# One 512-column matmul for both parts of x in the feed forwards' up products, and the bank's two halves added

## The chip, the cores and the metric

The kernel runs on one core of a Trainium2 chip. The metric is device time in microseconds from launch to end, the median of several runs. TensorE multiplies matrices and writes to PSUM, VectorE and ScalarE work elementwise, GpSimd does a few small operations, SyncE issues all DMA transfers.

## What is computed

A row of 256 tokens of width 1024 goes through three layers: differential attention with a pooling mixer, sliding window attention, and a block with a convolution module and gated attention. Four feed forwards of width 2816 belong to them; the first two convolve the up products over three tokens, the last two do not and add half of their result. The change touches these:

```python
def conv_glu_ffn(x, norm_g, w_up, conv_w, conv_b, w_down):
    S = x.shape[1]
    h = rms_norm(x, norm_g) @ w_up
    hp = jnp.pad(h, ((0, 0), (CONV_W - 1, 0), (0, 0)))
    c = conv_b
    for j in range(CONV_W):
        c = c + conv_w[j] * hp[:, j:j + S]
    gate, up = jnp.split(c, 2, axis=-1)
    return x + (jax.nn.silu(gate) * up) @ w_down

def swiglu_ffn(h, w13, w2):
    gate, up = jnp.split(h @ w13, 2, axis=-1)
    return (jax.nn.silu(gate) * up) @ w2
```

All of it is float32.

## The kernel before

**Products in parts.** Float32's accuracy comes from splitting. A weight chunk of 128x2048 is loaded by SyncE into one of two staging buffers `st` (line 175), ScalarE casts it to `whi` (line 191, two pieces of 1024 columns), and VectorE writes the remainder `wlo` (line 195, four pieces of 512). The normed and transposed x exists as two parts in the same way. A product is then three matmuls into one accumulation: first part by first part, first by second, second by first. `mm3` (lines 244 to 246) does this with tokens on the output's partitions and up to 512 columns of weights; `mm_w` (lines 462 to 464) does it with weights stationary and the 256 tokens as columns.

**Stream.** `Stream` holds five chunks of split weights. A chunk's buffer is released when TensorE has used it, then the next chunk is split into it and the staging buffer is loaded again. Its splitting has a low priority in the scheduler. A feed forward uses 22 chunks of up weights and 11 of down weights, in the order up, up, down in its steady part.

**Feed forward.** The up products are made in 22 blocks `f` of 128 gate columns and 128 up columns (the two halves `s`). Blocks 0 to 2 are "leads": made with tokens on partitions through `mm3`, copied to SBUF and transposed into a PSUM tile each (line 373). Blocks 3 to 21 come from `up_mm`: for each half, eight row blocks of x, three matmuls of 256 columns each. Both halves of a block stand in one PSUM tile `up` of 512 columns, that is one bank; the pool `ps` has four. `glu` then works on both halves: in the feed forwards with a convolution, ScalarE (line 398) and two VectorE steps (lines 399 and 401) a half, all reading `up`; then silu (407), product (409) and the two parts of `g` (413 and 414). Without a convolution silu and product read `up` themselves. After each second block, `down` multiplies two blocks of g by a down chunk into four accumulators `dn`: 24 matmuls of 512 columns. The last three chunks' down products come at the end, first for token block 0, then for token block 1, with the next stage's norm between them.

**Order.** Tiles are drawn from pools with a fixed number of buffers, and a scheduler puts the instructions of each engine into one fixed order, in which the engine then runs them; an instruction waits for semaphores of others. The pool `u` (`u288`, five buffers) gives the convolution's `c`.

## Time and profile before

| | us |
|---|---|
| median of three runs | 1078.18 |
| the three runs | 1079.1, 1074.94, 1078.18 |
| the profiled execution, first to last instruction (span) | 1077.6 |
| TensorE busy in it | 1052.6 |
| VectorE busy | 730.2 |
| ScalarE busy | 562.4 |

The profile is of one execution. Its span is the only time that is known of it. TensorE's matmuls overlap in the records, so its busy time and the mean of one matmul are longer than the share of the time that a matmul takes; distances between starts are free of that.

### The profile page before, as it was taken

How to read it: one execution, taken by the hardware profiler on the slowest of the kernel's cores; microseconds unless marked ns; L12 is line 12 of the kernel's file. 1: busy time of each engine (PE TensorE's matmuls, PEld its weight loads, DVE VectorE, ACT ScalarE, POOL GpSimd, SP SyncE). 2: the span in 40 equal slices, each digit the busy share in tenths (PEclk: the TensorE clock that was granted, in tenths of full speed). 3: DMA queues.
4: the chain of work that ended last, by engine and by line, in shares of the span. 5: the costliest groups of instructions: out<-in, count | busy, mean ns of one | idle time of the engine just before them, and what ended most of it. 6: DMA issues, size and time to landing. Idle time of an engine off the chain costs nothing.

```text
span 1077.6 us, 17590 instructions
## 1 busy us (share of the span) xinstructions
PE 1052.6 (98%) x7078; PEld 959.0 (89%) x7078; DVE 730.2 (68%) x1526; ACT 562.4 (52%) x953; POOL 32.0 (3%) x40
## 2 busy tenths in 40 slices
PE   5999999999999999999999999999999999999997
PEld 4778999999887898999999999999888889999996
DVE  5786787677867569777676555545799896545542
ACT  5575655555557457555555434433544566434431
POOL 1100000000021000000000000000000010000000
PEclk9999999999999999999999999999999999999999
DMA  6754565555453074555545555554613166555531
GB/s 248 249 192 157 182 229 195 182 180 189 157 176 118 1 248 167 205 186 192 195 158 186 203 184 190 195 180 173 203 71 118 40 215 235 194 183 174 193 118 39
DMA packets 28449, 185.82 MB, mean 172 GB/s; under 512 B 3280, under 2 KB 4176, under 8 KB 7120
## 3 DMA queue, kind: packets, MB, share of 16 engines
q1 hardware_dynamic: 28368, 184.71, 49.0%
q8 instruction: 55, 0.90, 0.3%
q14 instruction: 26, 0.21, 0.1%
HBM read 183.65 MB, written 1.05 MB: 171 GB/s over the span
## 4 chain that ended last, share of the span: by engine, by line
PE 88%; DVE 5%; DMA 4%; ACT 2%; issue 0%; POOL 0%; SPq 0%; POOLq 0%; ACTq 0%; DVEq 0%
PE up L464 13%; PE up L463 13%; PE up L462 13%; PE dn L244 7%; PE dn L245 7%; PE dn L246 7%; DMA st<-in_w 3%; PE sc L555 2%; PE op L244 2%; PE op L246 2%; PE op L245 2%; DVE wlo L195 2%; PE lead L246 2%; PE lead L244 2%; PE lead L245 2%; DVE ys L1008 2%
## 5 line engine op out<-in xcount | busy, mean ns | idle before, releaser
L195 DVE TENSOR_TENSOR wlo<-st,whi 128x512 fp32r<-128x512 f32 x668 | 435.4, 686 | 231.2 <-ACT whi L191 230.6
L191 ACT CAST whi<-st 128x1024 fp32r<-128x1024 f32 x334 | 342.6, 1046 | 316.2 <-PE up L463 180.6
L462 PE MATMUL up<-xT,whi 128*128 128x256 f32 x1216 | 344.6, 283 | 0.0
L464 PE MATMUL up<-xT,wlo 128*128 128x256 f32 x1216 | 344.1, 283 | 0.0
L463 PE MATMUL up<-xT,whi 128*128 128x256 f32 x1216 | 344.1, 283 | 0.0
L462 PEld LDWEIGHTS up<-xT,whi 128*128 128x128 f32 x1216 | 233.2, 192 | 1.3
L463 PEld LDWEIGHTS up<-xT,whi 128*128 128x128 f32 x1216 | 233.3, 192 | 1.2
L464 PEld LDWEIGHTS up<-xT,wlo 128*128 128x128 f32 x1216 | 233.2, 192 | 0.1
L244 PE MATMUL dn<-whi,g 128*128 128x512 f32 x352 | 137.9, 392 | 0.9 <-ACT g L413 0.9
L245 PE MATMUL dn<-wlo,g 128*128 128x512 f32 x352 | 137.4, 390 | 0.0
L246 PE MATMUL dn<-whi,g 128*128 128x512 f32 x352 | 137.2, 390 | 0.0
L246 PEld LDWEIGHTS dn<-whi,g 128*128 128x128 f32 x352 | 66.1, 188 | 15.1 <-DVE g L414 1.0
L244 PEld LDWEIGHTS dn<-whi,g 128*128 128x128 f32 x352 | 66.2, 188 | 13.8 <-ACT g L413 1.1
L245 PEld LDWEIGHTS dn<-wlo,g 128*128 128x128 f32 x352 | 66.2, 188 | 12.1
L398 ACT ACTIVATE c<-up,pv 128x256 f32<-128x256 f32 x88 | 49.6, 564 | 31.8 <-DVE c L401 27.2
L244 PE MATMUL lead<-whi,xT 128*128 128x256 f32 x192 | 55.3, 288 | 0.0
L246 PE MATMUL lead<-whi,xT 128*128 128x256 f32 x192 | 54.3, 283 | 0.0
L245 PE MATMUL lead<-wlo,xT 128*128 128x256 f32 x192 | 54.3, 283 | 0.0
L244 PE MATMUL proj<-whi,xT 128*128 128x512 f32 x112 | 46.1, 412 | 2.1 <-ACT xT L264 2.1
L246 PE MATMUL proj<-whi,xT 128*128 128x512 f32 x112 | 45.3, 404 | 0.3 <-DVE xT L265 0.3
L399 DVE SCALAR_TENSOR_TENSOR c<-up,pv,c 128x255 f32<-128x255 f32 x88 | 42.0, 477 | 4.4 <-ACT c L398 3.8
L1008 DVE SCALAR_TENSOR_TENSOR ys<-u,dwh,ys 128x240 f32<-128x240 f32 (+29 forms) x109 | 44.9, 460 | 0.1
(210 smaller groups left out, 1342.1 us busy)
## 6 DMA issues: line engine op xcount, KB each, us to landing
st<-in_up SPq DMA_DIRECT2D x88, 1024.0 KB, 4.9
st<-in_dn SPq DMA_DIRECT2D x44, 1024.0 KB, 4.8
st<-in_w SPq DMA_DIRECT2D x22, 1024.0 KB, 5.3
gb<-in_rows SPq DMA_DIRECT2D x10, 512.0 KB, 4.0
st<-in_w0o SPq DMA_DIRECT2D x4, 1024.0 KB, 5.0
st<-in_w1o SPq DMA_DIRECT2D x4, 1024.0 KB, 4.8
st<-in_w2o SPq DMA_DIRECT2D x4, 1024.0 KB, 4.8
st<-in_w SPq DMA_DIRECT2D x2, 512.0 KB, 8.0
```

The costliest lines, as they stand in the source:

```text
L191: A.copy(hi[:, c], st[:, c])
L195: V.tensor_sub(lo[:, c], st[:, c], hi[:, c].bitcast(F32))
L244: T.matmul(o, l[0], r[0], start=first, stop=False)
L245: T.matmul(o, l[0], r[1], start=False, stop=False)
L246: T.matmul(o, l[1], r[0], start=False, stop=last)
L398: A.activation(c, ps, AF.Identity, bias=PVs(cb, blk), scale=PVs(cw, 3 * blk + 2))
L399: V.scalar_tensor_tensor(c[:, 1:], ps[:, :S - 1], PVs(cw, 3 * blk + 1), c[:, 1:], ALU.mult, ALU.add)
L462: T.matmul(o, w[0], x[0], start=first, stop=False)
L463: T.matmul(o, w[0], x[1], start=False, stop=False)
L464: T.matmul(o, w[1], x[0], start=False, stop=last)
L555: T.matmul(o, qT[r0:r0 + 64, qb, :], kT[r0:r0 + 64, kb, 0:L], start=True, stop=extra is None)
L1008: V.scalar_tensor_tensor(y[:, k:], self.u[:, :S - k], self.w(k), y[:, k:], ALU.mult, ALU.add)
```

## The change

x's two parts become one tile with the parts side by side for every row block, so that 512 columns, 256 of each part, stand in a row. In `up_mm` each half gets a PSUM tile of its own. One matmul of 512 columns takes the weights' first part by both parts of x, into both halves of the bank; one of 256 columns adds the weights' second part by x's first part to the bank's first half. `join` then copies the bank's second half to SBUF on ScalarE and adds the first half to it on VectorE; `glu` reads these tiles `h` from SBUF. The `h` come from the pool `u`, with its five buffers as before. The leads, the down products and every other product keep their three matmuls; `mm_w` only takes its operand in another form. Lines move by 10 to 27.

```diff
+class Parts(tuple):
+    def __new__(cls, t):
+        self = super().__new__(cls, (t[:, :, 0, :], t[:, :, 1, :]))
+        self.t = t
+        return self
+    def both(self, ko):
+        return self.t[:, ko, :, :]
...
     def new_T(name):
-        return tuple(
-            act.tile([P, KD, S], F32R, tag=f"xT{k}", name=f"{name}{k}") for k in range(2)
-        )
+        return Parts(act.tile([P, KD, 2, S], F32R, tag="xT", name=name))
...
         def up_mm(self, f, mid=None):
-            o = self.ups[f] = ps_t("up").rearrange("p (s t) -> p s t", s=2)
+            hs = []
             w = v3(W.get(self.up, f), KD)
             for s in range(2):
                 if s and mid is not None:
                     mid()
+                o = ps_t("up")
                 for ko in range(KD):
-                    mm_w(o[:, s, :], cut(w, slice(None), ko, slice(s * P, (s + 1) * P)),
-                         cut(self.xT, slice(None), ko, slice(0, S)), ko == 0, ko == KD - 1)
+                    mm_both(o, cut(w, slice(None), ko, slice(s * P, (s + 1) * P)), self.xT, ko, ko == 0, ko == KD - 1)
+                hs.append(join(o))
             W.free((self.up, f))
-            self.glu(f)
-
-        def glu(self, f):
-            pu = self.ups.pop(f)
+            self.glu(f, hs)
+
+        def glu(self, f, hs=None):
+            if hs is None:
+                pu = self.ups.pop(f)
+                hs = [pu[:, s, :] for s in range(2)]
...
-                    ps = pu[:, s, :]
+                    ps = hs[s]
...
-                cs = [pu[:, s, :] for s in range(2)]
+                cs = hs
...
-    def mm_w(o, w, x, first, last):
+    def mm_w(o, w, xT, ko, first, last):
+        x = cut(xT, slice(None), ko, slice(0, S))
         T.matmul(o, w[0], x[0], start=first, stop=False)
         T.matmul(o, w[0], x[1], start=False, stop=False)
         T.matmul(o, w[1], x[0], start=False, stop=last)
+
+    def mm_both(o, w, xT, ko, first, last):
+        T.matmul(o, w[0], xT.both(ko), start=first, stop=False, skip_group_check=True)
+        T.matmul(o[:, :S], w[1], xT[0][:, ko, :], start=False, stop=last, skip_group_check=True)
+
+    def join(o):
+        h = u288("h")[:, :S]
+        A.copy(h, o[:, S:])
+        V.tensor_tensor(h, o[:, :S], h, ALU.add)
+        return h
```

The instructions' order shows it first on TensorE, at block 3 of the first feed forward, around the transposes of lead block 2 between its two halves. The first is the kernel before; the numbers in the names tell buffers apart.

```order
L463 MATMUL up_1207<-xT1_699,whi_899 128x256
L464 MATMUL up_1207<-xT0_698,wlo_902 128x256
L373 MATMUL up_1134<-cc_78,lead_1138 128x128 x2
L462 MATMUL up_1207<-xT0_698,whi_899 128x256
L463 MATMUL up_1207<-xT1_699,whi_899 128x256
```

The changed kernel at the same place on TensorE:

```order
L483 MATMUL up_1203<-xT_696,whi_896 128x512
L484 MATMUL up_1203<-xT_696,wlo_899 128x256
L383 MATMUL up_1130<-cc_78,lead_1134 128x128 x2
L483 MATMUL up_1240<-xT_696,whi_896 128x512
L484 MATMUL up_1240<-xT_696,wlo_899 128x256
```

The second half goes to a tile of its own, `up_1240`, the fifth of this pool since the leads; it takes the bank of lead block 0.

On ScalarE, in the steady part of the first feed forward, two successive blocks before (`c0` and `c1` are the two halves' convolution starts):

```order
L398 ACTIVATE c0_1575<-up_1516,pv_81 128x256
L191 CAST whi_1565<-st_1466 128x1024 x2
L398 ACTIVATE c1_1579<-up_1516,pv_81 128x256
L407 ACTIVATE sl_1583<-c0_1575 128x256
L413 CAST g_1587<-m_1585 128x256
L398 ACTIVATE c0_1649<-up_1590,pv_81 128x256
L191 CAST whi_1639<-st_1514 128x1024 x2
```

And two successive blocks on ScalarE in the changed kernel:

```order
L489 COPY h_1828<-up_1811 128x256
L203 CAST whi_1801<-st_1696 128x1024 x2
L489 COPY h_1848<-up_1831 128x256
L411 ACTIVATE c0_1861<-h_1828,pv_81 128x256
L411 ACTIVATE c1_1865<-h_1848,pv_81 128x256
L203 CAST whi_1851<-st_1761 128x1024 x2
L420 ACTIVATE sl_1869<-c0_1861 128x256
L489 COPY h_1893<-up_1876 128x256
L426 CAST g_1873<-m_1871 128x256
L489 COPY h_1913<-up_1896 128x256
```

Each half's copy now stands in the queue where the half ends, between the weight casts and the steps of `glu`, which read `h` in SBUF.

## Rows read from the trace of the kernel before

**Rows 1.** The page: TensorE's busy time, its granted clock by slices, the chain's shares.
```profile
PE 1052.6 (98%) x7078; PEld 959.0 (89%) x7078; DVE 730.2 (68%) x1526; ACT 562.4 (52%) x953; POOL 32.0 (3%) x40
...
PEclk9999999999999999999999999999999999999999
...
PE 88%; DVE 5%; DMA 4%; ACT 2%; issue 0%; POOL 0%; SPq 0%; POOLq 0%; ACTq 0%; DVEq 0%
```

**Rows 2.** Busy us of each engine by stretch, granted clock, DMA: two feed forwards.
```profile
125.00:285.00 160.00, 160.00 (x1128) 150.39 (x1127) 123.35 (x244) 92.20 (x144) 0.00 (x0) 1.00 0.55 190
...
592.00:755.00 163.00, 163.00 (x1142) 153.29 (x1141) 86.05 (x158) 69.75 (x101) 0.55 (x1) 1.00 0.54 187
```

**Rows 3.** Timeline of TensorE, first feed forward: start us, duration us, instruction.
```profile
196.77 0.40 PE L244 MATMUL dn<-whi,g 128*128 128x512 f32 x1
...
202.01 0.39 PE L246 MATMUL dn<-whi,g 128*128 128x512 f32 x1
202.24 0.28 PE L462 MATMUL up<-xT,whi 128*128 128x256 f32 x1
...
213.75 0.40 PE L244 MATMUL dn<-whi,g 128*128 128x512 f32 x1
```

**Rows 4.** Groups by line and shape: count, busy us, mean ns, idle before.
```profile
L462 PE MATMUL up<-xT,whi 128*128 128x256 f32 x1216 | 344.6, 283 | 0.0
...
L407 ACT ACTIVATE sl<-up 128x256 f32<-128x256 f32 x44 | 16.4, 379 | 7.9 <-PE up L464 7.8
...
L409 DVE TENSOR_TENSOR m<-up,sl 128x256 f32<-128x256 f32 x44 | 18.2, 418 | 7.7 <-ACT sl L407 7.7
...
L195 DVE TENSOR_TENSOR wlo<-st,whi 128x512 fp32r<-128x512 f32 x668 | 435.4, 686 | 231.2 <-ACT whi L191 230.6
...
L191 ACT CAST whi<-st 128x1024 fp32r<-128x1024 f32 x334 | 342.6, 1046 | 316.2 <-PE up L463 180.6 <-PE dn L246 61.3 <-DMA st<-in_w 27.6
...
L398 ACT ACTIVATE c<-up,pv 128x256 f32<-128x256 f32 x88 | 49.6, 564 | 31.8 <-DVE c L401 27.2 <-PE up L464 4.4
...
L413 ACT CAST g<-m 128x256 fp32r<-128x256 f32 x88 | 35.4, 404 | 16.0 <-DVE m L409 16.0
```

**Rows 5.** Timeline, first feed forward's start: block 3's products, block 0's last read, a wait.
```profile
122.61 0.36 PE L462 MATMUL up<-xT,whi 128*128 128x256 f32 x1
...
125.49 0.48 DVE L401 SCALAR_TENSOR_TENSOR c<-up,pv,c 128x254 f32<-128x254 f32 x1
...
129.18 0.19 PEld L246 LDWEIGHTS dn<-whi,g 128*128 128x128 f32 x1 [0.34 <-DVE g L414]
```

**Rows 6.** Timeline, second feed forward's start: the same places, with g's second part.
```profile
402.44 0.48 DVE L401 SCALAR_TENSOR_TENSOR c<-up,pv,c 128x254 f32<-128x254 f32 x1
...
405.64 0.42 DVE L414 TENSOR_TENSOR g<-m,g 128x256 fp32r<-128x256 f32 x1
...
406.12 0.19 PEld L246 LDWEIGHTS dn<-whi,g 128*128 128x128 f32 x1 [0.46 <-DVE g L414]
```

**Rows 7.** Timeline, first feed forward's end: last up product, first down product, a wait.
```profile
276.09 0.28 PE L464 MATMUL up<-xT,wlo 128*128 128x256 f32 x1
276.21 0.40 PE L244 MATMUL dn<-whi,g 128*128 128x512 f32 x1
...
283.39 0.19 PEld L246 LDWEIGHTS dn<-whi,g 128*128 128x128 f32 x1 [0.16 <-DVE g L414]
```

**Rows 8.** Weight stream, first feed forward: issues, a cast, landing us, ScalarE's waits.
```profile
195.51 0.33 SPq L175 DMA_DIRECT2D st<-in_up  x1
...
206.42 6.40 SPq L175 DMA_DIRECT2D st<-in_up  x2
...
202.44 1.05 ACT L191 CAST whi<-st 128x1024 fp32r<-128x1024 f32 x1 [1.19 <-PE dn L246]
...
st<-in_up SPq DMA_DIRECT2D x88, 1024.0 KB, 4.9
...
ACT whi L191 <- PE up L463: 30.1, 12, 3.3
```

More of the change, by code (lines that the diff above doesn't have):

```diff
@@ L979, in conv_in @@
                 mm_w(ag[j][:, s, :], cut(w, slice(None), ko, slice(s * P, (s + 1) * P)),
-                     cut(xT, slice(None), ko, slice(0, S)), ko == 0, ko == KD - 1)
+                     xT, ko, ko == 0, ko == KD - 1)
         W.free(("w2", j))
@@ L1031, in forget_sums @@
         for ko in range(KD):
-            mm_w(o, cut(flw, slice(None), ko), cut(xT, slice(None), ko, slice(0, S)), ko == 0, ko == KD - 1)
+            mm_w(o, cut(flw, slice(None), ko), xT, ko, ko == 0, ko == KD - 1)
         z, cum = (tmp.tile([P, S], F32, tag="sl", name=n)[:8, :] for n in ("z", "cum"))
@@ L1064, in proj_qk @@
             mm_w(o[:, :S], cut(v3(W.get("w2", 4 + 2 * s + ko // 4), 4), slice(None), ko % 4, slice(b * P, (b + 1) * P)),
-                 cut(xT, slice(None), ko, slice(0, S)), ko == 0, ko == KD - 1)
+                 xT, ko, ko == 0, ko == KD - 1)
         A.activation((q2, k2)[s][:, b, :], o[:, :S], AF.Copy, scale=1.0 if s else -0.125)
```

## The prediction

> **What bounds the kernel now.** I read the head of the page first [rows 1]: TensorE is busy 98% of the span, its granted clock is at full speed (the 2.4 GHz level) in all forty slices, and the chain that ended last runs 88% on it, with the three lines of the up products at the front of the list of lines. Busy time alone does not make an engine the bound here, since matmuls overlap and their ends are modelled, so I next read two feed forwards as stages [rows 2]. In the first TensorE has no idle time in 160 us, while VectorE is busy 77% and ScalarE 58%; in the third, which has no convolution, the others are at 53% and 43%. So in the feed forwards, some 640 of the 1078 us, the rate of the matmuls sets the time, and everything else has room.
>
> The mean of one up matmul, 283 ns in the groups by line [rows 4], is a duration in an overlapped pipeline and is of no use for a sum. The distance between starts is, and the timeline of TensorE gives it [rows 3]. Twenty-four down matmuls of 512 columns start between 196.77 and 202.24 us: 5.47 us, 227.9 ns each. Ninety-six up matmuls of 256 columns start between 202.24 and 213.75 us: 11.51 us, 119.9 ns each. Two equations, 512a + b = 227.9 and 256a + b = 119.9, give a = 0.4219 ns for a column (2.37 columns a ns, close to the clock) and b = 11.9 ns for each matmul whatever its width. That b is what the change can save, and only there.
>
> **What the change saves.** Each group of three 256-column matmuls on one weight block becomes one of 512 columns (first part of the weights, both parts of x) and one of 256 (second part of the weights, first part of x). The columns that stream stay 768. There are 1216 such groups (the count of line 462 [rows 4]: 4 feed forwards x 19 blocks x 2 halves x 8 row blocks). Before: 3 x 119.9 = 359.7 ns. After: 227.9 + 119.9 = 347.8 ns. Saved: 11.9 ns x 1216 = 14.5 us. Trains of one width are all that rows 3 measure, but the changes of width are there too: 512 followed by 256 takes 0.23 us (202.01 to 202.24 [rows 3]) and 256 followed by 512 takes 0.12 us (276.09 to 276.21 [rows 7]), so a mixed pair should cost the sum of its parts, and not more. One weight load of the three goes as well; it overlaps the matmuls before and after, so I price it at nothing beyond b. Bounds on the term: nothing, if an alternating pair costs what three did, and 29 us, if the pair's shorter matmul loses its b as well; I take 14.5 us, from the rows that measure both widths. A loss is excluded by the 0.23 and 0.12 us.
>
> The Trainium skill, page "TensorE: Matmul & The Clock Gate", section "Back-to-back issue gap", gives the warm gap as the columns at 2.4 GHz plus about 2.5 ns. By that rule b is 2.5 and the change saves an estimated 1216 x 2.5 = 3.0 us, which would leave the time near 1075 us; the trace does not agree, with 11.9 ns.
>
> **What the change adds.** Per half, a ScalarE copy out of the bank's second 256 columns and a VectorE addition of the first: 152 of each. Nearest rows [rows 4]: the silu that reads 128x256 from PSUM takes 379 ns, the product that takes one operand from PSUM and one from SBUF takes 418 ns. A feed forward gets 38 of each: ScalarE + 14.4 us, VectorE + 15.9 us. In the first feed forward's stage that makes VectorE 123.35 + 15.9 = 139 of about 156 us (89%) and ScalarE 107 of 156 (68%): off the path, since neither reaches the bound, but with less room. What covers it is the queue of finished work ahead of TensorE. The order of the DMA issues, of GpSimd's instructions and of those of the stages between the feed forwards stays as it was, so there I change nothing.
>
> **Banks.** Before, a block's two halves share one of four PSUM banks, which comes free after the last of the convolution's reads; now each half has a bank of its own, which comes free after its copy and its addition. TensorE therefore comes back to a bank after three more halves, 3 x 8 x 347.8 ns = 8.3 us, where it had three whole blocks, over 17 us. In the steady order the copy follows a half directly or stands behind two convolution starts, a pair of weight casts and a silu (2 x 564, 2 x 1046, 379 ns [rows 4]), and the addition behind one or two weight subtractions (686 ns each): 3.6 + 0.4 + 1.4 + 0.4 = 5.8 us at most. That fits 8.3 us, so I price it at nothing.
>
> It does not fit at the start of the two feed forwards with a convolution. There the first three blocks still hold three banks, the first half of block 3 takes the fourth, and its second half needs the bank of block 0, which six operations must first read; before, the second half went on in its own bank. In the first feed forward the products of block 3 start at 122.61 us and the last read of block 0 ends at 125.49 + 0.48 = 125.97 us [rows 5]. Sixteen matmuls (2.78 us) and two transposes end at about 125.6, so TensorE waits some 0.4 us, starts the second half at 126.0 and the down products at 128.8. The third of these started at 129.18 before, already behind the same VectorE result [rows 5]; now it is about 129.26. In the second feed forward block 0 is read until 402.44 + 0.48 = 402.92 us [rows 6]; the second half then runs to 405.7, and the third down product, held before until 406.12 by the second part of g (405.64 + 0.42 = 406.06), comes at 406.2. So the two starts lose about 0.1 us each and the 0.19 us that block 3 would have saved: 0.6 us together. Without a convolution two operations read a lead's bank, and I see no wait.
>
> **The end of a feed forward** gets shorter, not longer. Block 21's last product starts at 276.09 us; the second part of its g releases a weight load at 283.39, which has waited 0.16 us for it [rows 7]. After the change the first half's join runs beside the second half. Behind the last product ScalarE has the copy, a convolution start, a cast of g, a weight cast and the second convolution start (0.38 + 0.56 + 0.40 + 1.05 + 0.56 = 2.95 us [rows 4]); VectorE then two convolution steps (0.48 each [rows 5]), two weight subtractions and the product (2.75 us in all), and last come the cast of g and its subtraction, 0.82 us: 6.5 us against 7.1 us. I take 0.16 us off.
>
> **The sum**, against the profiled execution: 1077.6 - 14.5 + 0.6 - 0.2 = 1063.5 us of span. The median of the three runs is 0.6 us above that span, so the forecast is 1064 us.
>
> **The rivals.**
> First, the pair saves nothing: the fixed part hangs on changing between widths or on the long matmul's doubled operand, and 512 + 256 columns take the 359.7 ns that three matmuls took. Then only the starts' 0.2 us are left and the time is about 1078 us, no change. Against it stand the two changes of width above, at 0.23 and 0.12 us; for it, that no train of alternating pairs is in the trace. The Trainium skill's rule of "Back-to-back issue gap", with its fixed part of 2.5 ns, leads to nearly the same place; the 11.9 ns speak against it.
>
> Second, a slower kernel: the bank hand-over takes the matmuls' place as the bound. The place is the copy in ScalarE's queue. A weight cast waits there for TensorE to finish with an older chunk, 12 times by line 463 in the first feed forward and up to 3.3 us at once [rows 8]; a copy behind it waits too. 3.3 + 2.1 for the pair of casts + 0.4 copy + two subtractions 1.4 + 0.4 addition is 7.6 us, 0.7 short of the 8.3 at which TensorE starts to stand. A pair of convolution starts ahead of the copy (2 x 0.56 us) makes it 8.7: 0.4 us at half of the 152 halves is 30 us, and the time 1094 us. The gain is gone from 0.1 us per half on. Against it: the waits of ScalarE for TensorE end with the very product that the copy behind them needs, or an earlier one, so they are mostly not added to the copy's own wait.
>
> Third, half the gain: the weight stream falls behind. One staging buffer goes round in 206.42 - 195.51 = 10.9 us [rows 8]: issued at 195.51, landed 4.9 us later at 200.4, its cast starts at 202.44 on a release by TensorE, 2.0 us of room. Two chunks now take 0.25 us less, and a join in the stretch from cast to last subtraction adds about 0.8 us, so 1 us of room stays; if two or three joins fall there (2.1 us), each round is 0.3 us late, 16 rounds make 5 us in a feed forward. The five live chunks absorb that in part, so I put this case at 3 to 9 us lost, 1067 to 1073 us.
>
> Fourth, more gain than 15 us, if the 256-column matmul in the pair hides its fixed part wholly under the long one: twice 14.5 us, 1049 us. Nothing in rows 3 asks for it.
>
> **How the numbers follow.** Forecast (1061 to 1067 us) 0.76; half the gain 0.10; nothing saved 0.06; slower by the banks 0.05; twice the gain 0.03. The kernel's own three runs lie between 1074.9 and 1079.1 us, so I let the lower end of the forecast go down by 2 us, to 1059; the upper end, 1071, takes in the better half of the third rival. What is left out is 0.03 + 0.06 + 0.05 + 0.05 = 0.19. A measurement of this kernel tells about 0.5% (5.4 us) from no change, so faster means below 1072.8 us: 0.76 + 0.03 + 0.08 = 0.87. No change: 0.06 + 0.02 = 0.08. Slower: 0.05.
>
> **What would show it.** In the changed kernel's timeline one half's matmuls should start 2.78 us behind the other's, with about 228 ns after each 512-column matmul and 120 ns after each 256-column one; 240 ns after the long one would be the first rival. TensorE should show no wait for the additions in the steady part of any feed forward, and one of about 0.4 us and 1.6 us ahead of the second half of block 3 in the first and second feed forward; waits of the up products for VectorE all along would be the second rival, and casts that wait for a DMA of up or down weights in place of TensorE the third. VectorE's busy time should rise by about 64 us and ScalarE's by about 58. The stretches between the feed forwards should keep their lengths. What would make the prediction wrong is a fixed part that is not b of rows 3, or a copy that regularly reaches its bank more than 8 us late.

## The result

| | before | after |
|---|---|---|
| median, us | 1077.56 (1074.94 to 1079.1, 5 runs) | 1070.18 (1069.44 to 1073.31, 5 runs) |
| ratio, 95% interval | | 0.9939, 0.9922 to 0.9956 |
| span of the profiled execution, us | 1077.6 | 1070.6 |
| VectorE busy, us | 730.2 | 777.9 |
| ScalarE busy, us | 562.4 | 619.1 |

The kernel became 0.6% faster. The direction was right, and the time lies just inside the stated range; the size was not right: 7 us came where 14 were forecast. What follows is about the missing half.

The page after answers to [rows 1] with TensorE's busy line, its granted clock (nine tenths or more, the level of 2.4 GHz, in all slices but one, which shows eight) and the chain:

```profile
PE 1046.3 (98%) x5862; PEld 894.8 (84%) x5862; DVE 777.9 (73%) x1678; ACT 619.1 (58%) x1105; POOL 32.0 (3%) x40
...
PEclk9999999999999999999999999999998999999999
...
PE 87%; DVE 5%; DMA 3%; ACT 2%; issue 1%; POOL 1%; SPq 0%; POOLq 0%; ACTq 0%; DVEq 0%
```

TensorE executes 1216 matmuls fewer and still sets the time. The two stretches of [rows 2], as the busy time of each engine after (us, PE, PEld, DVE, ACT, POOL, then clock, DMA share, GB/s):

```profile
125.00:285.00 160.00, 159.04 (x831) 135.14 (x830) 134.02 (x283) 106.10 (x185) 0.00 (x0) 1.00 0.55 190
592.00:755.00 163.00, 163.00 (x850) 138.74 (x849) 102.32 (x199) 86.46 (x140) 0.55 (x1) 1.00 0.54 186
```

VectorE has 134 of 160 us to do in the first and ScalarE 106, both below the span, as the prediction had it. In the third feed forward TensorE has no idle time at all. So the answer lies in its rate. The timeline of TensorE at the entry of a group of pairs, in the same feed forward as [rows 3] (start us, duration us, instruction):

```profile
184.66 0.39 PE L258 MATMUL dn<-whi,g 128*128 128x512 f32 x1
184.88 0.39 PE L483 MATMUL up<-xT,whi 128*128 128x512 f32 x1
185.11 0.28 PE L484 MATMUL up<-xT,wlo 128*128 128x256 f32 x1
185.22 0.40 PE L483 MATMUL up<-xT,whi 128*128 128x512 f32 x1
185.45 0.28 PE L484 MATMUL up<-xT,wlo 128*128 128x256 f32 x1
185.57 0.40 PE L483 MATMUL up<-xT,whi 128*128 128x512 f32 x1
185.81 0.28 PE L484 MATMUL up<-xT,wlo 128*128 128x256 f32 x1
185.93 0.40 PE L483 MATMUL up<-xT,whi 128*128 128x512 f32 x1
```

From 184.88 to 185.93 us three pairs take 1.05 us. The trace holds the starts in nanoseconds, and there one pattern repeats every three pairs: 241 and 119, 236 and 113, 233 and 117 ns behind the long and the short matmuls, 1059 ns in all, 353 a pair. (Distances below a nanosecond here and below are means over many such starts.) Before, three matmuls took 360.0 ns. So 7 ns a pair were saved, and not 11.9.

The length of the stages, read from TensorE's starts: first lead product to first down product, from there to the last up product, from there to the last down product.

| us | before, feed forwards 1 to 4 | after |
|---|---|---|
| start | 25.17, 26.24, 25.18, 25.18 | 26.22, 25.49, 24.99, 25.54 |
| steady part | 147.45, 147.68, 147.24, 147.24 | 145.52, 145.53, 145.52, 145.54 |
| end | 17.20, 17.21, 17.13, 16.24 | 17.32, 17.33, 17.14, 16.23 |

The steady parts give 7.5 us, the starts lose 0.5 and the ends 0.2; the rest of the span is 0.2 us shorter. Of the 7.5 us some 0.6 are waits and not rate: before, the first two steady parts were 0.2 and 0.4 us longer than the other two, with the waits for g of [rows 5] and [rows 6] in them, and after all four are equal. The steady part is the finest measure there is of the change: in the changed kernel it repeats to 0.02 us over four feed forwards, where the stretch between the third and the fourth took anything from 118.7 to 124.5 us in the profiles of this study, whatever the kernel, and moves single times by some us.

The groups by line that answer to [rows 4] (count, busy us, mean ns, idle before):

```profile
L483 PE MATMUL up<-xT,whi 128*128 128x512 f32 x1216 | 431.4, 399 | 1.5 <-DVE c L414 1.2
L484 PE MATMUL up<-xT,wlo 128*128 128x256 f32 x1216 | 341.7, 281 | 0.0
...
L489 ACT COPY h<-up 128x256 f32<-128x256 f32 x152 | 55.8, 367 | 56.8 <-PE up L484 56.6
L490 DVE TENSOR_TENSOR h<-up,h 128x256 f32<-128x256 f32 x152 | 63.7, 419 | 10.2 <-ACT h L489 10.0
L203 ACT CAST whi<-st 128x1024 fp32r<-128x1024 f32 x334 | 343.1, 1048 | 176.9 <-PE up L483 66.0 <-PE dn L258 42.0 <-DMA st<-in_up 20.1
```

The joins cost ScalarE 55.8 and VectorE 63.7 us, and neither the up products nor the casts show a wait for them that matters: all 2432 matmuls of both lines waited 1.5 us together.

### The profile page after: what moved, and what is told of

The parts are those of the page before. It is cut to its first block, busy times and chain, and to the rows that moved or that the text cites. A ratio compares the mean times of both kernels' runs of the same rounds, so it can differ in the third digit from the quotient of the medians.

```text
span 1070.6 us, 15476 instructions
## 1 busy us (share of the span) xinstructions
PE 1046.3 (98%) x5862; PEld 894.8 (84%) x5862; DVE 777.9 (73%) x1678; ACT 619.1 (58%) x1105; POOL 32.0 (3%) x40
## 3 DMA queue, kind: packets, MB, share of 16 engines
HBM read 183.65 MB, written 1.05 MB: 173 GB/s over the span
## 4 chain that ended last, share of the span: by engine, by line
PE 87%; DVE 5%; DMA 3%; ACT 2%; issue 1%; POOL 1%; SPq 0%; POOLq 0%; ACTq 0%; DVEq 0%
PE up L483 26%; PE up L484 13%; PE dn L256 8%; PE dn L258 7%; PE dn L257 7%; PE sc L582 2%; DVE wlo L207 2%; DMA st<-in_w 2%; PE proj L256 2%; PE proj L258 2%; PE proj L257 2%; PE o L841 1%; PE op L256 1%; PE op L257 1%; PE op L258 1%; DMA st<-in_up 1%
## 5 line engine op out<-in xcount | busy, mean ns | idle before, releaser
L207 DVE TENSOR_TENSOR wlo<-st,whi 128x512 fp32r<-128x512 f32 x668 | 441.6, 686 | 179.6 <-ACT whi L203 178.9
L483 PE MATMUL up<-xT,whi 128*128 128x512 f32 x1216 | 431.4, 399 | 1.5 <-DVE c L414 1.2
L483 PEld LDWEIGHTS up<-xT,whi 128*128 128x128 f32 x1216 | 228.6, 188 | 58.0 <-issue 1.6
L484 PEld LDWEIGHTS up<-xT,wlo 128*128 128x128 f32 x1216 | 230.3, 189 | 1.3
L489 ACT COPY h<-up 128x256 f32<-128x256 f32 x152 | 55.8, 367 | 56.8 <-PE up L484 56.6
L256 PEld LDWEIGHTS dn<-whi,g 128*128 128x128 f32 x352 | 66.1, 188 | 14.5 <-ACT g L426 0.6
L490 DVE TENSOR_TENSOR h<-up,h 128x256 f32<-128x256 f32 x152 | 63.7, 419 | 10.2 <-ACT h L489 10.0
L426 ACT CAST g<-m 128x256 fp32r<-128x256 f32 x88 | 35.5, 406 | 28.3 <-DVE m L422 28.3
L284 ACT ACTIVATE junk<-x 128x512 bf16<-128x512 f32 x32 | 20.2, 631 | 47.2 <-DVE x L323 26.1
L411 ACT ACTIVATE c<-h,pv 128x256 f32<-128x256 f32 x76 | 45.8, 603 | 2.4 <-DVE h L490 2.4
```

Of the source, the lines that this page charges most:

```text
L207: V.tensor_sub(lo[:, c], st[:, c], hi[:, c].bitcast(F32))
L256: T.matmul(o, l[0], r[0], start=first, stop=False)
L411: A.activation(c, ps, AF.Identity, bias=PVs(cb, blk), scale=PVs(cw, 3 * blk + 2))
L426: A.copy(hi, m)
L483: T.matmul(o, w[0], xT.both(ko), start=first, stop=False, skip_group_check=True)
L484: T.matmul(o[:, :S], w[1], xT[0][:, ko, :], start=False, stop=last, skip_group_check=True)
```

## The experiments

Theories at the start: **A**, changing between widths costs TensorE time that trains of one width don't show; **B**, the long matmul's operand or x's new layout costs; **C**, the traffic of the joins to and from PSUM slows the matmuls. Each run has the kernel before beside it on the same chip, at medians of 1076.5 to 1078.4 us.

### Runs of eight and of sixteen (e1_runs8, e2_runs16)

The same matmuls in another order: eight long ones, then eight short ones in each half; then sixteen long ones into two banks, then sixteen short ones (block 3 stays in pairs there).

```diff
                 for ko in range(KD):
-                    mm_both(o, ...)
+                    mm_long(o, cut(w, ...), self.xT, ko, ko == 0)
+                for ko in range(KD):
+                    mm_short(o, cut(w, ...), self.xT, ko, ko == KD - 1)
```

Expected of eight:

> The changed kernel with the order inside each half altered: eight 512-column matmuls in a row, then eight of 256 columns. Same matmuls, loads, banks and joins. Theory A, a change of width costs: in the changed kernel a 512-column matmul between two of 256 takes 236 ns and the short one 117 ns, 353 ns a pair; in the down products, the first long ones after a run of short ones take 233, 236, 228, 233, 231 ns and then settle at 227. So the long ones here should mean some 230 ns and the short ones 120, 350 ns a pair, and the time should fall by about 1216 x 3 ns = 4 us, to 1066 us. Theory B, the long matmul of the up products costs 236 ns by its own operands (x as the moving operand, both parts, one bank's two halves): every long one stays at 236, the time stays at 1070 us. Theory C, the joins' traffic slows the matmuls: as B, 1070 us.

Expected of sixteen:

> The changed kernel with both halves of a block taken together (all but block 3): sixteen 512-column matmuls into two banks, then sixteen of 256 columns, then the two joins. Theory A, change of width: fewer changes than with runs of eight, long ones mean some 228.5 ns, 348.5 ns a pair over 1152 pairs, about 5.5 us less than the changed kernel, 1064.5 us, unless the later join of the first half makes a wait. Theories B and C: 353 ns a pair, 1070 us, no gain over the changed kernel.

Measured: 1064.84 us (ratio 0.989, 0.9859 to 0.9922) and 1062.82 us (0.9888, 0.9834 to 0.9942). The steady parts are 143.96 and 143.61 us. Timeline of TensorE, runs of eight; equal matmuls in a row are one row with their count:

```profile
250.99 1.98 PE L483 MATMUL up<-xT,whi 128*128 128x512 f32 x8
252.80 1.12 PE L486 MATMUL up<-xT,wlo 128*128 128x256 f32 x8
253.76 2.00 PE L483 MATMUL up<-xT,whi 128*128 128x512 f32 x8
255.60 1.11 PE L486 MATMUL up<-xT,wlo 128*128 128x256 f32 x8
```

Runs of sixteen:

```profile
189.04 3.82 PE L490 MATMUL up<-xT,whi 128*128 128x512 f32 x16
192.69 0.52 PE L493 MATMUL up<-xT,wlo 128*128 128x256 f32 x3
```

The view of the runs of sixteen ends inside its second run.

The run at 250.99 us comes straight from down products, which are 512 wide too: eight in 1.81 us, 226 ns each. The next one, behind short ones, takes 1.84 us. In means by position the long ones take 232, 233, 228, 231, 230 ns and then 226.7 for as long as the run lasts; the short ones 113, 119 and then 120.0. The whole comes to 348.4 ns a pair in runs of eight and 347.2 in runs of sixteen. The operands and the joins are as in the changed kernel, and with runs of eight the banks too, so the order alone is worth 5 to 7 us. The same long matmul runs at 226.7 ns here, so B's operand falls.

### The layout alone, and no joins (e3_layout, e4_nojoin)

The kernel before with x's parts side by side in one tile; and the changed kernel without the joins, which leaves the product of the weights' first part and x's second part out of blocks 3 to 21.

```diff
     def new_T(name):
-        return tuple(
-            act.tile([P, KD, S], F32R, tag=f"xT{k}", name=f"{name}{k}") for k in range(2)
-        )
+        return Parts(act.tile([P, KD, 2, S], F32R, tag="xT", name=name))
```

```diff
-                hs.append(join(o))
+                hs.append(o[:, :S])
```

> The kernel before with one thing of the change: the two parts of x side by side in one tile. Three 256-column matmuls, one bank for both halves, no join. If the layout slowed the reads of x (a part of theory B), the 256-column matmuls would take more than the 120 ns of the kernel before, and 3 x 1216 of them at, say, 122 ns would add 7 us, 1085 us. Theories A and C: 120 ns, no change from the kernel before, 1077.6 us.

> The changed kernel without its joins: the silu and the convolution read the bank's first half, so the product of the weights' first part by x's second part is left out of the result. TensorE's instructions and banks are the same; 152 copies and 152 additions are gone. Theory C, the joins' traffic slows the matmuls: the pair falls from 353 to some 347 ns, the time by 7 us to 1063 us. Theories A and B: the pair stays at 353 ns and the time within 1 us of the changed kernel's, 1069.5 us, with what is left from the starts of the feed forwards.

Measured: 1078.38 us (0.9994, 0.9976 to 1.0011) and 1071.32 us (0.9945, 0.9924 to 0.9966). Timeline of TensorE with the layout alone, three matmuls apart:

```profile
188.69 0.28 PE L472 MATMUL up<-xT,whi 128*128 128x256 f32 x1
...
189.05 0.28 PE L472 MATMUL up<-xT,whi 128*128 128x256 f32 x1
```

And without joins, one pair:

```profile
188.90 0.40 PE L483 MATMUL up<-xT,whi 128*128 128x512 f32 x1
189.14 0.28 PE L484 MATMUL up<-xT,wlo 128*128 128x256 f32 x1
189.25 0.40 PE L483 MATMUL up<-xT,whi 128*128 128x512 f32 x1
```

The three matmuls take 0.36 us as before (120.0 ns each), and the steady parts without joins are 145.52, 145.54, 145.52 and 145.52 us, those of the changed kernel to 0.02. B's layout and C fall.

### Two equal widths, and 512 with 384 (e5_wide, e9_384)

Is it the change of width, or the alternation of two weight blocks behind a 512-column matmul? Both kernels widen the second matmul only, and so add products of the two second parts.

```diff
-        T.matmul(o[:, :S], w[1], xT[0][:, ko, :], ...)
+        T.matmul(o, w[1], xT.both(ko), ...)
```

```diff
-        T.matmul(o[:, :S], w[1], xT[0][:, ko, :], ...)
+        T.matmul(o[:, : S + P], w[1], xT.both(ko).rearrange("p a s -> p (a s)")[:, : S + P], ...)
```

> Both matmuls of a pair 512 columns wide: the second one takes the weights' second part by both parts of x, which adds the product of the two second parts that the other kernels leave out. In the up products and the down products no matmul has another width than the one before it; the stationary block still alternates between the weights' first and second part. Theory A (a change of width costs): 226.7 to 228 ns between all starts, as in the trains of the down products, 454 to 456 ns a pair against 353 in the changed kernel, so 1216 x 0.102 = about 124 us more, near 1194 us. Rival D (the alternation between two stationary blocks costs, at 512 columns, whatever the width that follows): 236 ns each, 472 ns a pair, 1216 x 0.119 = 145 us more, near 1215 us.

> The second matmul of a pair made 384 columns wide: it also takes the weights' second part by the first 128 columns of x's second part, products that the other kernels leave out. The widths alternate as in the changed kernel, 512 and 384, but no matmul is near the 109 to 112 ns at which trains of 64 and 128 columns run in the kernel before, so that cadence of weight loads can't be felt. Theory A (a change of width costs, whatever the narrower width): more than the settled 226.7 + 173.3 = 400.0 ns a pair, near 406 (the 6.2 ns of the changed kernel's pairs): from the first down product to the last up product 145.5 + 288 x 0.053 = 160.8 us, the whole near 1134 us. Rival E (the short one is too near the weight load's cadence, and the matmul after it pays): 400.0 ns a pair, 159.1 us, the whole near 1127 us.

Measured: 1188.89 and 1132.41 us. Both timelines of TensorE, first 512 with 512:

```profile
188.82 0.39 PE L484 MATMUL up<-xT,wlo 128*128 128x512 f32 x1
189.05 0.39 PE L483 MATMUL up<-xT,whi 128*128 128x512 f32 x1
189.27 0.39 PE L484 MATMUL up<-xT,wlo 128*128 128x512 f32 x1
```

And 512 with 384:

```profile
190.03 0.40 PE L483 MATMUL up<-xT,whi 128*128 128x512 f32 x1
190.26 0.34 PE L484 MATMUL up<-xT,wlo 128*128 128x384 f32 x1
190.43 0.39 PE L483 MATMUL up<-xT,whi 128*128 128x512 f32 x1
```

Both are single runs, read by their rates. Without a change of width every step is 226.8 ns in the mean, though the weight blocks alternate. With 384 it is 231.7 + 174.9 = 406.6 ns a pair against 400.0 in settled trains: the same 6.6 ns, with a narrower matmul far above the 109 to 112 ns at which the kernel before runs trains of 64 and 128 columns, by its starts. So alternating widths are needed for the loss, and neither the alternation of weight blocks by itself nor a short matmul near that 109 to 112 ns is what it comes from. Whether the weight loads have a part in it otherwise no run shows.

### Runs of two and of four (e6_runs2, e10_runs4)

```diff
-                for ko in range(KD):
-                    mm_both(o, ...)
+                for k2 in range(0, KD, 2):
+                    for ko in (k2, k2 + 1):
+                        mm_long(o, cut(w, ...), self.xT, ko, ko == 0)
+                    for ko in (k2, k2 + 1):
+                        mm_short(o, cut(w, ...), self.xT, ko, ko == KD - 1)
```

> Runs of two: two long matmuls, then two short ones. Theory A with a fixed price for each change of width (in pairs 353.0 - 346.7 = 6.3 ns there and back): half of the changes, 349.8 ns a pair, 1216 x 0.0032 = 3.8 us less than the changed kernel, about 1066.5 us. Theory A' (not the change, but the first few long ones after it are dear, as in the runs of eight, where the long ones took 231.8, 233.4, 228.1, 231.3, 229.8 and then 226.8 ns): the second long one is still dear, so the pair stays near 352 ns, under 1.5 us less, about 1069 us.

> Runs of four long and four short. The excess over settled trains was 6.2 ns for one long and one short, 2.8 ns for a run of two and two, 13.7 ns for eight and eight, 8.0 ns for sixteen and sixteen. If a change there and back has a price between those of two and of eight, 347.4 to 350.1 ns a pair, and the stretch from the first down product to the last up product is 143.4 to 144.3 us (runs of two: 143.75, of eight: 143.96, of sixteen: 143.6). If the excess falls with the length of the run, 143.4 or less.

Measured: 1062.15 us (0.9853, 0.983 to 0.9877) and, in one run, 1066.59 us. Timeline of TensorE, runs of two:

```profile
189.52 0.63 PE L484 MATMUL up<-xT,whi 128*128 128x512 f32 x2
189.99 0.40 PE L487 MATMUL up<-xT,wlo 128*128 128x256 f32 x2
190.22 0.63 PE L484 MATMUL up<-xT,whi 128*128 128x512 f32 x2
```

Two pairs take 0.70 us (189.52 to 190.22). The means are 348.1 ns a pair in runs of two (steady part 143.75 us) and 350.0 in runs of four (144.6). Both forecasts for runs of two missed, 349.8 and 352; with runs of four the pair lies in the stated 347.4 to 350.1 ns, the steady part above the stated 144.3 us. The excess over settled trains, for one change there and back, is 6.2 ns in pairs, 2.8 in runs of two, 13 in runs of four, 14 of eight and 8 of sixteen. That is no price per change, and A in its simple form fell here.

### What the rows of the changed kernel already held, and a test of it (e12_phase)

The first half of block 3 runs in the same pairs, and it is the one place that starts behind a break in TensorE's stream: two transposes and a step of about 0.3 us. Timeline of TensorE after, first feed forward:

```profile
122.36 0.40 PE L483 MATMUL up<-xT,whi 128*128 128x512 f32 x1
...
124.44 0.40 PE L483 MATMUL up<-xT,whi 128*128 128x512 f32 x1
...
126.12 0.47 PE L483 MATMUL up<-xT,whi 128*128 128x512 f32 x1 [0.96 <-DVE c L414]
```

Six pairs in 2.08 us: 346.7 ns each, the sum of the settled steps, with nothing lost. All four feed forwards show this in that half; in the second half, behind a break of another length, two show it and two show 353. **Theory F**: the same alternation has two patterns, and the offset at which it starts, in time against the work ahead, decides between them. The test puts one more matmul ahead of every second block, of nine different widths; the next matmul overwrites its result.

```diff
                 o = ps_t("up")
+                if mid is None and s == 0 and f % 2 == 0:
+                    n = S + 8 * (f - 4)
+                    T.matmul(o[:, :n], cut(w, slice(None), 0, slice(0, P))[0],
+                             self.xT.both(0).rearrange("p a s -> p (a s)")[:, :n], start=True, stop=False, ...)
```

> The changed kernel with one matmul more ahead of each second block (4, 6, ... 20): the weights' first part by 256, 272, 288, ... 384 columns of x, nine widths in the nine places of a feed forward; its result is overwritten by the next matmul. The pairs then start at nine different offsets to the work ahead of them. In the changed kernel's trace all groups of 32 pairs cost 197 ns more than settled trains (353 ns a pair), but the eight pairs of block 3's first half cost nothing more (346.7 ns a pair), and those of its second half 0 or 45 ns; these halves alone come after a break in TensorE's stream, two transposes and about 0.3 us. Theory A (the alternation costs by itself, in a stream without a break): 353 ns a pair in all nine places, the same excess of about 197 ns. Theory F (the offset at which the pairs start decides it): some of the nine places run at 346.7 ns, at the same widths in all four feed forwards. Time: 36 more matmuls of 320 columns on average, about 147 ns each, 5.3 us: 1075 to 1076 us under A, down to 1069 us under F.

Measured: 1073.09 us in one run. Timeline of TensorE behind the matmul of 304 columns:

```profile
184.48 0.30 PE L396 MATMUL up<-xT,whi 128*128 128x304 f32 x1
184.62 0.39 PE L488 MATMUL up<-xT,whi 128*128 128x512 f32 x1
...
185.31 0.39 PE L488 MATMUL up<-xT,whi 128*128 128x512 f32 x1
...
185.66 0.39 PE L488 MATMUL up<-xT,whi 128*128 128x512 f32 x1
```

And behind the one of 336 columns, two places on:

```profile
217.88 0.31 PE L396 MATMUL up<-xT,whi 128*128 128x336 f32 x1
218.03 0.40 PE L488 MATMUL up<-xT,whi 128*128 128x512 f32 x1
...
219.08 0.40 PE L488 MATMUL up<-xT,whi 128*128 128x512 f32 x1
```

Three pairs take 1.04 us in the first (184.62 to 185.66) and 1.05 in the second (218.03 to 219.08). The difference of 19 ns is small in such rows; in the starts, over all pairs of a place, it is plain:

| columns of the added matmul | 256 | 272 | 288 | 304 | 320 | 336 | 352 | 368 | 384 |
|---|---|---|---|---|---|---|---|---|---|
| ns a pair, third feed forward | 353.4 | 353.3 | 353.4 | 346.8 | 346.7 | 353.0 | 353.0 | 346.7 | 347.0 |
| ns a pair, fourth | 353.5 | 353.3 | 353.4 | 346.8 | 346.7 | 353.0 | 353.0 | 346.8 | 347.0 |

The first two feed forwards repeat the eight values from 272 on within 0.1 ns (in their first place down products fall in between). There are two rates and nothing between them, and four places out of nine alternate through 32 pairs and lose nothing: alternation by itself (A) does not cost. Each width has one place here, so this run alone does not tell width from place; the next ones do. The place of 384 columns is also not like the others: it lies in the middle of the last group and is entered from pairs, which run fast here, where the others are entered from down products. Theory F fits; that the offset in time decides, and not something else that goes with the width, is argued and not shown.

### Does a place keep its pattern, and can it be had for nothing (e13_once, e14_each, e15_swap)

One matmul of 304 columns at block 4 alone; one ahead of every second block; and, without any added work, two long and two short ones at the same places before the pairs go on.

```diff
+                if mid is None and s == 0 and f == 4:
+                    n = 304
+                    ...
```

```diff
+                if mid is None and s == 0 and f % 2 == 0:
+                    n = 304
+                    ...
```

```diff
+                k0 = 2 if mid is None and s == 0 and f % 2 == 0 else 0
+                for ko in range(k0):
+                    mm_long(o, cut(w, ...), self.xT, ko, ko == 0)
+                for ko in range(k0):
+                    mm_short(o, cut(w, ...), self.xT, ko, False)
-                for ko in range(KD):
+                for ko in range(k0, KD):
                     mm_both(o, ...)
```

> The changed kernel with one matmul of 304 columns more per feed forward, ahead of block 4 alone; its result is overwritten by the next matmul. Theory F1 (the offset is carried on through the down products, which are trains of settled matmuls): all groups of pairs of the feed forward run at 346.7 ns, from the first down product to the last up product 145.5 + 0.14 - 288 x 0.0063 = 143.8 us, 6.8 us less in all, about 1063.5 us. Theory F2 (each group of pairs finds its pattern anew at its entry): only the groups up to the first down products behind block 4 change, 0.2 us a feed forward, and the matmul costs 0.14: about 1070 us, as the changed kernel.

> The same matmul of 304 columns ahead of every second block (4, 6, ... 20), nine in a feed forward. If 304 columns give the good offset to whatever went before, all places run at 346.7 ns: 145.5 - 9 x 0.2 + 9 x 0.136 = 144.9 us from the first down product to the last up product, about 1068 us. If the offset adds up from place to place, some places run at 353 ns, in a pattern that repeats over the places, and the stretch is 145.5 to 146.5 us.

> No work is added: in the first half of every second block (4, 6, ... 20) the first two row blocks run as two long and two short matmuls, the other 14 halves' row blocks and the rest as pairs. Whether this order gives the good offset can't be told from the rows; theory F says that every place is at one of the two rates, about 346.7 or 353 ns a pair, so the stretch from the first down product to the last up product is 143.7 us (about 1063 us in all) or 145.5 us (1070 us). Without theory F it is 145.4 us, a few changes of width fewer.

Measured: 1072.3 us (0.9951, 0.9919 to 0.9984), 1072.73 us (0.9953, 0.9935 to 0.9971) and 1068.59 us (0.9926, 0.99 to 0.9951). Timeline of TensorE with one matmul, third feed forward, six pairs of its place and then six of the next place behind down products:

```profile
597.65 0.39 PE L488 MATMUL up<-xT,whi 128*128 128x512 f32 x1
...
599.73 0.39 PE L488 MATMUL up<-xT,whi 128*128 128x512 f32 x1
...
614.22 0.40 PE L488 MATMUL up<-xT,whi 128*128 128x512 f32 x1
...
616.34 0.40 PE L488 MATMUL up<-xT,whi 128*128 128x512 f32 x1
```

They take 2.08 and 2.12 us. In the third and the fourth feed forward the pairs of that place run at 346.8 ns up to the next down products, and at 352.8 in every place behind them. In the first two the down products come after a single pair, and already the other 30 pairs of the place run at 353.3. So a train of 24 down matmuls brings the stream back to where it was, and each entry decides anew. With one matmul at each place, all places that it separates from down products run at 346.8 ns, whatever the place, where without it they run at 353: the width decides, and not the place. Only the one in the middle of the last group, which is entered from pairs, falls back to 353. The steady parts are 145.0 to 145.2 us: the pairs gain 0.2 us a place, and the 136 ns of the added matmul take most of it back. The median of 1072.73 us, where about 1068 was expected, does not show this gain.

The swap does not change the pattern in the places that are entered from down products (352.7 ns over the place). In the last one, entered from pairs, it does. Timeline of TensorE, third feed forward, six pairs of an earlier place, and six behind the swap in the last one:

```profile
704.32 0.40 PE L488 MATMUL up<-xT,whi 128*128 128x512 f32 x1
...
706.44 0.40 PE L488 MATMUL up<-xT,whi 128*128 128x512 f32 x1
...
724.24 0.40 PE L488 MATMUL up<-xT,whi 128*128 128x512 f32 x1
...
726.32 0.40 PE L488 MATMUL up<-xT,whi 128*128 128x512 f32 x1
```

The first six take 2.12 us and the second 2.08. By the starts, the 30 pairs behind the swap in that place run at 346.7 ns in all four feed forwards, without any added work. The trains of down products behind the other places take 227.8 ns a matmul in place of the changed kernel's 229.3. Each of the two is worth about half of the 0.5 us that the swap gains in the steady part. An entry from down products that costs nothing and gives 346.8 was not found.

### The start, and the best versions (e7_start, e8_best, e11_runs2s)

Block 3 the old way (one bank for both halves, three matmuls of 256 columns): alone; with runs of sixteen, and of eight in block 21; with runs of two.

```diff
+            if mid is not None:
+                o = self.ups[f] = ps_t("up").rearrange("p (s t) -> p s t", s=2)
+                for s in range(2):
+                    if s:
+                        mid()
+                    for ko in range(KD):
+                        mm_w(o[:, s, :], ...)
+                W.free((self.up, f))
+                self.glu(f)
+                return
```

> The changed kernel with block 3, the first of up_mm, made the old way: one bank for both halves, three matmuls of 256 columns. If the starts lose what the waits for block 0's bank show, the waits of the up products for VectorE's c vanish and the stretch from the first lead to the first down product goes from 25.5 to 26.2 us back to about 25.2 in the feed forwards with a convolution: 0.5 to 1.5 us in all, 1069 to 1070 us. If that stretch is set by VectorE's work on the leads anyway, it stays at 25.5 or more.

> Blocks 4 to 20 with sixteen long matmuls into two banks, then sixteen short ones; block 21 with eight and eight a half; block 3 the old way. Theory A: 226.7 ns long and 120.0 ns short in the runs, with a few dear long ones once a block, so from the first down product to the last up product about 143.7 us, as with runs of sixteen (143.6), the end of the second feed forward back from 18.45 to 17.3 us, the starts 25.2: about 1061 us. If runs of sixteen and of eight differ by nothing, 1063 to 1065 us.

> Runs of two, and block 3 the old way, in one bank with three matmuls of 256 columns. If the waits at the two starts are what the fourth bank costs, the start stretches are 25.2 us (25.0 to 25.5 with runs of two alone) and the rest stays at 143.75 and 17.15: 743.1 us for the four feed forwards instead of 743.7, about 1061.5 us; no difference from runs of two (1062.15) that a measurement can tell.

Measured: 1071.82 us (0.9958, 0.9933 to 0.9982), 1061.19 us (0.985, 0.9818 to 0.9883) and 1062.7 us (0.9862, 0.9838 to 0.9885). The starts are 25.17 to 25.18 us in all three. The median of the first shows no gain over the changed kernel's 1070.18. The end of the second feed forward, 18.45 us with runs of sixteen throughout (e2_runs16), is 17.18 with runs of eight in block 21. But the waits moved and did not vanish. The weight load of the third down product, in e7_start:

```profile
128.51 0.19 PEld L258 LDWEIGHTS dn<-whi,g 128*128 128x128 f32 x1 [0.34 <-DVE g L438]
```

It waits 0.34 us for g's second part, as in [rows 5]. The steady parts of the two feed forwards with a convolution are 145.73 and 145.75 us against 145.52 and 145.53. So of the 0.33 us that the second one's start gained (25.49 to 25.17), 0.2 come back at once; the first one's start of 26.22 is no measure, since kernels with the same start (e12_phase, e15_swap) took 25.50 and 25.51 there. The wait for VectorE's g stands at this place with block 3 the old way, as it did before. The versions with runs of two, of sixteen, and both with block 3 the old way lie at 1061.2 to 1062.8 us with overlapping intervals; by the medians each beats the changed kernel by 7 to 9 us, and which is best can't be told.

## Why the prediction was right and wrong

**What bounds the kernel**: right. TensorE's matmul rate sets the feed forwards' time; nothing done to the other engines (e4_nojoin) moved the steady part.

**What the change saves**: this is the step that failed. It said that a mixed pair "should cost the sum of its parts, and not more", because 512 followed by 256 took 0.23 us and 256 followed by 512 took 0.12 [rows 3, 7]. The term was 14.5 us. In the mean of the steady parts a pair saved 359.8 - 352.9 = 6.9 ns, which is 8.4 us over 1216 pairs and 8.0 over the 1152 of the steady parts, and the down products behind them lost 1.0 us of it (the mean step of their trains of 24 went from 227.8 to 229.2 ns); with the 0.6 us of waits that left, that comes to the 7.5 within 0.1. What the pairs met is the slower of the two patterns, 353 ns, which e1_runs8, e12_phase and e14_each show to hang on the order and the entry and not on the matmuls themselves. Two readings were too coarse. Rows of 0.01 us hide 6 ns, which is half of the 11.9 at stake. And the change shows not in the one step at the border but in the following ones: in the kernel before, the down matmuls behind a train of short ones took 233, 236, 228, 233, 231 and only then 227 ns, so the mean of 227.9 over 24 [rows 3] was itself a mixture (and the short ones behind long ones began with 113 and 119). Settled steps are 226.7 and 120.0 ns, which makes the fixed part 13.3 ns and not 11.9 (256 columns more take 106.7 ns, and 120.0 - 106.7 = 13.3): the saving that the prediction was after is real, even larger, and pairs get it at some entries and not at the entry from down products that nearly all of this kernel's pairs have.

The rule of the Trainium skill that was weighed there (page "TensorE: Matmul & The Clock Gate", section "Back-to-back issue gap") sets a fixed 2.5 ns above the columns, and the page gives it for the isolated matmul. It does not describe these trains, which have 13.3 ns; the estimate of 3.0 us by it lies below the measured 8.4 us, and the forecast's 14.5 above.

**What it adds**: right. ScalarE's copies take 55.8 us and VectorE's additions 63.7, the forecast's 58 and 64, and without them the steady part is the same to 0.02 us. VectorE's busy time rose by 47.7 us in place of 64. The durations of its instructions, summed, rose by 64.7 us (824.3 to 889.0): where two records overlap, busy time counts the stretch only once.

**Banks**: no wait in the steady part, as said. At the starts the wait was there, 0.96 us in the first feed forward (forecast 0.4) and 0.28 in the second (forecast 1.6); in e12_phase and e13_once, which start alike, it was 0.3 in both. The net was forecast as 0.6 us and measured as 0.5; but these starts change by up to 1 us from profile to profile (the second is 26.24 us before and 25.17 in e3_layout, whose work is the same), so the agreement says little.

**The end**: wrong in sign. The two ends with a convolution grew by 0.12 us each, where 0.16 less was forecast. Without the joins (e4_nojoin) they take 17.15 and 17.14 us in place of 17.32 and 17.33, so the joins cost them some 0.2 us.

**The rivals.** The first (nothing saved) looked at the right place, the alternation of widths, and expected twice the loss; it is not a price of changing between widths, since pairs behind another entry lose nothing. Its mark of 240 ns behind the long matmul against the forecast's 228 was not reached: the mean is 236. The third gave 1067 to 1073 us, and the time is in it, but not by its mechanism. The upper end of the stated range, 1071, was set for the sake of this rival; that the time lies inside it is luck. The waits of ScalarE for the stream after, with count and longest:

```profile
ACT whi L203 <- PE up L483: 66.0, 53, 2.3
...
ACT whi L203 <- DMA st<-in_up: 20.1, 18, 2.9
```

Casts wait less for TensorE than before (66.0 us by this line, 180.6 by line 463 in [rows 4]) and little more for the loads, and TensorE waits for neither in the steady part. The second and the fourth rival did not come.

## What to carry to other kernels

A saving per instruction must be read from a stream of the new shape, not from two trains of the old ones: where instructions of two sizes will alternate, look in nanosecond starts at the first five or ten behind each change of size, and take the fixed part from settled steps only. When a merged matmul gives half of what the count says, try the order before anything else: runs of two, eight or sixteen of one width cost no work, and here gave another 5 to 8 us by the medians. A cost that depends on the order need not be a price per change; vary the entry before believing one.

## What the runs showed of the hardware that was not expected

Float32 matmuls with a weight load each settle at 120.0 ns (256 columns) and 226.7 ns (512) here, 13.3 ns above 2.4 columns a ns. Alternating 512 and 256 columns runs in one of two patterns, 346.7 ns a pair, or 353 in a pattern that repeats every three pairs, and keeps it through at least 32 pairs; which one depends on what stands just ahead of it. Between down products and pairs, a single matmul of 304, 320 or 368 columns gave the fast one, of 256, 272, 288, 336 or 352 the slow one. Entered from pairs, 384 columns behind fast pairs kept the fast one, 304 behind fast pairs gave the slow one, and two long and two short matmuls behind slow pairs gave the fast one. A train of 24 matmuls of 512 columns undid the effect (e13_once). Why there are two patterns is not settled: the slow one's excess is some 6.3 ns a pair, and no run shows what TensorE does in it.
